# A transformer block on one core: dummy matmuls on ones at the start, tokens split straight from PSUM, and norms spread by a matrix of ones

## The chip, the cores and the metric

The kernel runs on one core of one Trainium2 chip, in one launch. The metric is device time in microseconds, the median of several executions. A profile is one further execution, recorded by the hardware profiler; its span is a little shorter than the device time of the same execution. The engines are called PE (TensorE matmul), PEld (its weight load), DVE (VectorE), ACT (ScalarE), POOL (GpSimd) and SP (SyncE, which starts DMAs).

## The reference

One transformer block over 528 tokens (16 learned meta tokens ahead of 512 real ones) of width 1024, all in float32:

```python
h = concat([meta, x])                                   # 528 x 1024
h = h + 0.5 * swiglu(rmsnorm(h, ffn1_norm), w_gate, w_up, w_down)   # d_ff = 2816
h = h + hybrid_mixer(rmsnorm(h, mix_norm))
h = h + 0.5 * swiglu(rmsnorm(h, ffn2_norm), w_gate2, w_up2, w_down2)
return rmsnorm(h, final_norm)[16:]

rmsnorm(x, g) = x * rsqrt(mean(x*x, -1) + 1e-6) * g
swiglu(u, ...) = (silu(u @ w_gate) * (u @ w_up)) @ w_down
```

The mixer projects the normed tokens with one wide matrix, runs a retention of 4 heads (keys of 256, values of 512, each head's output normed by its own root mean square, then gated) and an attention of 8 heads over 16 meta tokens and 128 keys chosen by an index score, gates and adds both, and projects them back.

## The kernel before

**Layout.** Activations lie with the features on the partitions and the tokens along the free dimension, so 1024 features are 8 tiles `hT[k]` of 128 x 528. Every matmul is made of three: each float32 operand is split into a `hi` part rounded to the PE's float32r form and a `lo` part with the rest, and `mm3` issues hi x hi, hi x lo and lo x hi for each of the 8 slices. ACT makes the `hi` part and another engine (DVE, if nothing else is said) the `lo` part, once for each weight (`split_w`, 1024 columns per partition) and once for each activation tile (`split`, or `split_gain`, which multiplies by the norm's gain on the way). A product over 528 tokens is issued in two parts (`halves`), each in a bank of its own of a two-bank PSUM tile. There are four such tiles in the first feed-forward stage.

**Norms.** The gain is folded into the activations as they are split; the factor per token is applied behind the product, when a PSUM tile is read: `R` is a 128 x 528 tile with the token's factor on every partition. `rstd_steps` makes it. It is a generator, so that its caller can put other matmuls between its steps: (1) PE sums `ssum` (the squares, already added over the 8 tiles by DVE or POOL) over the partitions by matmuls against a column of ones, which gives one column per 128 tokens; DVE scales it and POOL raises it to the power -0.5, which gives `rcol`; (2) PE transposes `rcol` and DVE copies the rows out, which gives `rrow`; (3) PE multiplies, for each 128 tokens, a column of the identity, broadcast, by these rows, which puts a row's factors on all partitions; ACT copies the result out of PSUM. The function is called seven times: for the first norm (`psr`), for the mixer's (`psn`, R2), for the output of each of the four retention heads (`rn`), and for the norm of the second feed-forward stage (R3).

**The start.** SP loads the tokens in five pieces by rows of tokens (`xt0` to `xt4`; sides[0] is the first 256 tokens, sides[1] the other 272) and, between them, the first two gate weights of 128 columns each. `token_half(h, k0)` transposes two feature slices of one side into a PSUM tile, copies both to `hT` (ACT or DVE in turn), and splits them from there. The first side's four pairs come first; then PE goes through the first gate tile's eight slices for the first 256 tokens, and after every second slice it transposes a pair of the second side. The two weights' `lo` parts are made by POOL here. Then the squares of all `hT` are added up, the second gate tile is run for the first 256 tokens, both tiles for the other 272, and the first up tile begins (`psu`), with the three steps of the norm between its parts. From there the two feed-forward halves (12 and 10 tiles of 128 hidden features) run gate, up and down.

**Order.** PE's instructions go in the order of the program text. The instructions of the other engines are ordered by a scheduler when the program is built, from its own estimate of when each is ready, and are then issued in that fixed order. Each engine waits on semaphores where it needs another's result. Tiles of one `tag` share a number of buffers (`bufs`), and a new tile waits until the oldest user of its buffer is done. `tmp()` is such a shared scratch tile of 128 x 528; the norm's callers in the mixer already use it.

Of the kernel before, what the change touches and what calls it, by code (L numbers as in the profile page):

```python
# [18 lines left out]
P = 128  # L19
D = 1024  # L20
KD = D // P
S = 512
# [59 lines left out]
def kernel(ctx: ExitStack, tc: tile.TileContext, x, meta, g1, wg1, wu1, wd1, gm,  # L82
# [11 lines left out]
    def pool(name, bufs=1, space=None, side=None):  # L94
        kw = {} if space is None else {"space": space}
        if side is not None:
            kw["side"] = side
        return tc.tile_pool(name=name, bufs=bufs, reuse_waits="tile", **kw)
# [7 lines left out]
    make_identity(nc, ident)  # L106
    ones = cpool.tile([P, 1], F32, name="ones")
    nc.gpsimd.memset(ones, 1.0)
    mhalf = cpool.tile([P, 5], F32, name="mhalf")
    nc.gpsimd.memset(mhalf, -0.5)  # L110
    gains = cpool.tile([P, 3, KD], F32, name="gains")
# [68 lines left out]
    def xs(k):  # L180
        return xs_now[k]
# [3 lines left out]
    def halves(t, cut=TH):  # L185

        a, b = t[:, 512 - cut : 512], t[:, 512 : 512 + T - cut]
        return [(a, slice(0, cut)), (b, slice(cut, T))], t[:, 512 - cut : 512 - cut + T]

    def rstd_steps(ssum, n, dim, dst, sp, psum):  # L190

        ends = [min(b * P, n - P) for b in range(-(-n // P))]
        nb = len(ends)
        col = psum()
        for b, t0 in enumerate(ends):
            nc.tensor.matmul(col[:, b : b + 1], ssum[:, t0 : t0 + P], ones, start=True, stop=True)
        ms = sp.tile([P, 5], F32, tag="ms", name="ms", bufs=2)
        nc.vector.tensor_scalar(ms[:, :nb], col[:, :nb], 1.0 / dim, EPS, ALU.mult, ALU.add)
        r = sp.tile([P, 5], F32, tag="rcol", name="rcol", bufs=2)
        nc.gpsimd.tensor_tensor(r[:, :nb], ms[:, :nb], mhalf[:, :nb], ALU.pow)  # L200
        yield True
        rows = psum()
        nc.tensor.transpose(rows[:nb, 0:P], r[:, :nb], ident)
        rs = sp.tile([5, P], F32, tag="rrow", name="rrow")
        nc.vector.tensor_copy(rs[:nb, :], rows[:nb, 0:P])
        yield True
        ps = psum()
        for b, t0 in enumerate(ends):
            t1 = min(b * P + P, n)
            nc.tensor.matmul(ps[:, b * P : t1], ident[:nb, b : b + 1].to_broadcast([nb, P]), rs[:nb, b * P - t0 : t1 - t0],  # L210
                             start=True, stop=True)
        nc.scalar.activation(dst, ps[:, :n], AF.Copy)  # L212
        yield False

# [24 lines left out]
    with pool("f1") as fp, pool("f1ps", 4, PSUM) as mmp:  # L239
        def mm_tile(name):  # L240
            return mmp.tile([P, 1024], F32, tag="mm", name=name)
# [8 lines left out]
            nc.tensor.transpose(pg[:, : n * KD], grow[n - 1], ident[: n * KD, : n * KD])  # L250
            nc.vector.tensor_copy(gains[:, i : i + n, :].rearrange("p a k -> p (a k)"), pg[:, : n * KD])

        hT2 = [fp.tile([P, 2, T], F32, tag=f"hT{k}", name=f"hT{k}") for k in range(KD // 2)]
        hT = [hT2[k // 2][:, k % 2, :] for k in range(KD)]
        sides = [[(0, P), (P, P)], [(2 * P, P), (3 * P, P), (4 * P, NM)]]
        bounds = [b for side in sides for b in side]
        sts = ExitStack()
        st_pool = sts.enter_context(pool("st"))
        xt, first_raw = [], []
        for b, (t0, n) in enumerate(bounds):  # L260
            t = st_pool.tile([n, D], F32, tag=f"xt{b}", name=f"xt{b}")
# [9 lines left out]

        CUT0 = 2 * P

        def token_half(h, k0):
            hs = (slice(0, CUT0), slice(CUT0, T))[h]
            w = hs.stop - hs.start
            ps = mm_tile("pst").rearrange("p (a b) -> p a b", a=2)
            for k in (k0, k0 + 1):
                for b, (t0, n) in enumerate(sides[h]):
                    nc.tensor.transpose(ps[:, k % 2, b * P : b * P + n], xt[2 * h + b][:, k * P : (k + 1) * P],  # L280
                                        ident[:n, :n])
            pair = hT2[k0 // 2][:, :, hs]
            if k0 % 4:
                nc.scalar.activation(pair, ps[:, :, :w], AF.Copy)
            else:
                nc.vector.tensor_copy(pair, ps[:, :, :w])
            for k in (k0, k0 + 1):
                xh, xl = xs(k)
                split_gain(hT[k][:, hs], gains[:, 0, k : k + 1], xh[:, hs], xl[:, hs])

        for k in range(KD):
            new_x(k)
        gains_in(0, 1)
        for k in range(0, KD, 2):
            if k == 0:
                first_w = split_w(first_raw[0], nc.gpsimd)
            token_half(0, k)
        pss = [mm_tile("psg") for _ in range(1)]
        for k in range(KD):
            mm3(halves(pss[0], CUT0)[0][:1], [w[:, k : k + 1, :] for w in first_w], lambda _: xs(k), 1, k == 0, k == KD - 1)  # L300
            if k % 2:
                token_half(1, k - 1)
            if k == 1:
                next_w = split_w(first_raw[1], nc.gpsimd)
        sts.close()
        hidp = sts.enter_context(pool("hid"))
        ssum = fp.tile([P, T], F32, tag="ssum", name="ssum")
        for k in range(KD):
            add_square(hT[k], ssum, k == 0, fp, bufs=4, eng=nc.vector)

        for f0, nf in ((0, 12), (12, 10)):
            hid = []
            for f in range(f0, f0 + nf, 2):
                cg = slice(f * P, (f + 2) * P)
                if f:
                    raw = load_w(wg1[:, cg], KD, 2 * P)
                    pss = []
                    for i in range(2):
                        w = split_w(raw[:, :, i * P : (i + 1) * P])
                        ps = mm_tile("psg")  # L320
                        mm3(halves(ps)[0], w, xs, KD)
                        pss.append(ps)
                else:
                    pss.append(mm_tile("psg"))
                    mm3(halves(pss[1], CUT0)[0][:1], next_w, xs, KD)
                    for p_, w in zip(pss, (first_w, next_w)):
                        mm3(halves(p_, CUT0)[0][1:], w, xs, KD)
                    psr = mm_tile("psr")
                    norm = rstd_steps(ssum, T, D, R, fp, lambda: psr)
                    raw = load_w(wu1[:, cg], KD, 2 * P)  # L330
                    w0 = split_w(raw[:, :, :P])
                    ps0 = mm_tile("psu")
                    part = halves(ps0)[0]
                    mm3(part[:1], [w[:, :4, :] for w in w0], xs, 4, True, False)
                    next(norm)
                    mm3(part[:1], [w[:, 4:, :] for w in w0], lambda k: xs(k + 4), 4, False, True)
                    mm3(part[1:], [w[:, :4, :] for w in w0], xs, 4, True, False)
                    next(norm)
                    mm3(part[1:], [w[:, 4:, :] for w in w0], lambda k: xs(k + 4), 4, False, True)
                    next(norm)  # L340
                st = []
                for i in range(2):
                    t = fp.tile([P, T], F32, tag="t", name="t", bufs=3)
                    nc.vector.tensor_tensor(t, halves(pss[i], TH if f else CUT0)[1], R, ALU.mult)
                    nc.scalar.activation(t, t, AF.Silu)  # L345
                    nc.gpsimd.tensor_tensor(t, t, R, ALU.mult)  # L346
                    st.append(t)
                if f:
                    raw = load_w(wu1[:, cg], KD, 2 * P)
                for i in range(2):  # L350
                    if f + i == 0:
                        ps = ps0
                    else:
                        w = split_w(raw[:, :, i * P : (i + 1) * P])
                        ps = mm_tile("psu")
                        mm3(halves(ps)[0], w, xs, KD)
                    if f + i == 1:
                        gains_in(1, 2)
                    pr = fp.tile([P, T], F32, tag="pr", name="pr", bufs=2)
                    nc.vector.tensor_tensor(pr, halves(ps)[1], st[i], ALU.mult)  # L360
                    hh = hidp.tile([P, TX], F32R, tag=f"hh{f - f0 + i}", name="hh")[:, :T]
                    hl = hidp.tile([P, TX], F32R, tag=f"hl{f - f0 + i}", name="hl")[:, :T]
                    split(pr, hh, hl)
                    hid.append((hh, hl))
# [38 lines left out]

    def mm_tile(name):
        return mmp.tile([P, 1024], F32, tag="mm", name=name)

    tp = {}

    def tmp():
        return tp["pool"].tile([P, T], F32, tag="tmp", name="tmp", bufs=tp["bufs"])  # L410

    def rope_swap(ps, cos, sin, half, n):

# [479 lines left out]
    ssum3 = hpool.tile([P, S], F32, tag="ssum3", name="ssum3")  # L893
    R3 = hpool.tile([P, S], F32, tag="R3", name="R3")
    with pool("om") as ou:
        def to_tokens(c, hc):
            ps = sm_tile("psht")
            for b in range(4):
                nc.tensor.transpose(ps[:, b * P : (b + 1) * P], hc[:, b * P : (b + 1) * P], ident)
            for b in range(4):  # L900
                nc.scalar.activation(hTok[b][:, c * P : (c + 1) * P], ps[:, b * P : (b + 1) * P], AF.Copy)
# [150 lines left out]
```

## Time and profile before

| | |
|---|---|
| median of 3 runs | 1612.23 us (1612.2 to 1612.44) |
| profiled execution | 1612.07 us, span 1610.2 us |
| mean granted PE clock | 0.994 |
| PE | 1590.3 us busy (99%), 9772 matmuls |
| DVE, ACT, POOL | 816.0, 564.7 and 238.9 us busy (51%, 35%, 15%) |
| DMA | 148.66 MB, mean 92 GB/s |
| instructions | 23061 |

How the views are read. The page's strip shows the span in 40 slices, one digit each; the clock digit is the share of full TensorE speed that was granted. A table of windows gives, for each stretch of time, each engine's busy time and instruction count, the granted clock and the DMA. The chain is the work that ended last, followed back from the end: each piece was released by the one before it. A group line gives line, engine, operation, output and inputs, shapes and count, then busy time and the mean duration of one in ns, then the idle time before it and who ended it. The duration of a pipelined matmul is longer than its distance to the next, so paces are taken from a piece of the chain divided by its count. In names, `whi` and `wlo` are a weight's two parts, `xh` and `xl` an activation tile's, `pst` a PSUM tile of transposed tokens, and `psg`, `psu`, `psd` products of gate, up and down.

### The profile page before, as it was taken

The numbers are of one execution on the slowest core, as the hardware profiler recorded it, in microseconds if no ns is written. First come the engines' busy times: TensorE is split into PE (matmuls) and PEld (weight loads), VectorE is DVE, ScalarE is ACT, GpSimd is POOL, SyncE is SP. The second block draws the span as 40 slices with busy tenths as digits, with TensorE's granted clock in tenths as the row PEclk, the third lists the DMA queues.
The fourth block names the chain that finished last, engine by engine and source line by source line (L and its number), as shares of the span: only waits on it lengthen the run. The fifth ranks groups of instructions, "written<-read, shape, count | busy, mean of one in ns | idle before, by whom it ended". The sixth has DMA issues, their size and how long they took to land.

```text
span 1610.2 us, 23061 instructions
## 1 busy us (share of the span) xinstructions
PE 1590.3 (99%) x9772; PEld 1429.6 (89%) x9772; DVE 816.0 (51%) x1256; ACT 564.7 (35%) x897; POOL 238.9 (15%) x186
## 2 busy tenths in 40 slices
PE   7999999999999999999999999999999999999998
PEld 6999999999888889889888999988888888888886
DVE  4333333334485686776844667653454343333434
ACT  4322222224543323233233555553234332212323
POOL 2111001101320200301303300111002211001100
PEclk7999999999999999999999999999999999999999
DMA  5232233224342032231312422222343323233222
GB/s 165 80 101 70 90 108 98 87 66 149 100 136 69 27 128 66 80 101 53 119 52 66 119 66 66 83 76 82 102 137 99 110 87 105 79 106 104 92 84 86
DMA packets 148262, 148.66 MB, mean 92 GB/s; under 512 B 3224, under 2 KB 137392, under 8 KB 148160
## 3 DMA queue, kind: packets, MB, share of 16 engines
q1 hardware_dynamic: 143632, 138.23, 26.8%
q10 hardware_dynamic: 4464, 8.96, 1.6%
q8 instruction: 76, 1.25, 0.3%
q14 instruction: 26, 0.21, 0.0%
q0 software_dynamic: 64, 0.01, 0.0%
HBM read 143.00 MB, written 4.19 MB: 91 GB/s over the span
## 4 chain that ended last, share of the span: by engine, by line
PE 95%; DVE 2%; DMA 1%; ACT 1%; POOL 1%; issue 1%; SPq 0%; ACTq 0%; POOLq 0%; DVEq 0%
PE psg L150 16%; PE psu L150 15%; PE psd L150 8%; PE psd L1013 7%; PE psrv L150 6%; PE psrg L150 5%; PE psro L150 4%; PE psrk L150 3%; PE psrq L150 3%; PE psgate L150 3%; PE psmo L150 3%; PE psat L150 3%; PE psga L150 3%; PE psak L150 3%; PE psav L150 3%; PE psaq L150 2%
## 5 line engine op out<-in xcount | busy, mean ns | idle before, releaser
L115 ACT ACTIVATE whi<-raw 128x1024 fp32r<-128x1024 f32 (+3 forms) x283 | 277.7, 982 | 875.3 <-PE psu L150 171.7
L116 DVE TENSOR_TENSOR wlo<-raw,whi 128x1024 fp32r<-128x1024 f32 (+3 forms) x281 | 336.0, 1196 | 176.5 <-ACT whi L115 172.9
L150 PE MATMUL psg<-xl,whi 128*128 128x264 f32 (+3 forms) x528 | 144.1, 323 | 1.9 <-DVE xl L120 1.9
L150 PE MATMUL psg<-xh,whi 128*128 128x264 f32 (+3 forms) x528 | 145.5, 325 | 0.4 <-ACT xh L119 0.4
L150 PE MATMUL psg<-xh,wlo 128*128 128x264 f32 (+3 forms) x528 | 143.9, 322 | 0.0
L150 PE MATMUL psu<-xh,whi 128*128 128x264 f32 (+1 forms) x528 | 141.4, 319 | 0.7 <-ACT R L212 0.7
L150 PE MATMUL psu<-xl,whi 128*128 128x264 f32 (+1 forms) x528 | 140.6, 318 | 0.0
L150 PE MATMUL psu<-xh,wlo 128*128 128x264 f32 (+1 forms) x528 | 140.4, 318 | 0.0
L150 PEld LDWEIGHTS psg<-xl,whi 128*128 128x128 f32 x528 | 90.9, 192 | 8.9 <-DVE xl L120 2.1
L150 PEld LDWEIGHTS psg<-xh,whi 128*128 128x128 f32 x528 | 90.1, 192 | 7.6 <-ACT xh L119 0.6
L150 PEld LDWEIGHTS psg<-xh,wlo 128*128 128x128 f32 x528 | 90.5, 192 | 6.9
L150 PEld LDWEIGHTS psu<-xh,whi 128*128 128x128 f32 x528 | 87.5, 188 | 7.8 <-ACT R L212 0.8
L150 PEld LDWEIGHTS psu<-xl,whi 128*128 128x128 f32 x528 | 88.1, 188 | 6.8
L150 PEld LDWEIGHTS psu<-xh,wlo 128*128 128x128 f32 x528 | 87.8, 188 | 6.9
L346 POOL TENSOR_TENSOR t<-t,R 128x528 f32<-128x528 f32 x22 | 37.5, 1708 | 263.8 <-ACT t L345 263.8
L988 POOL TENSOR_TENSOR t<-t,R 128x512 f32<-128x512 f32 x22 | 38.1, 1735 | 253.4 <-ACT t L987 253.4
L150 PE MATMUL psd<-hh,whi 128*128 128x264 f32 x352 | 71.3, 284 | 0.0
L150 PE MATMUL psd<-hl,whi 128*128 128x264 f32 x352 | 70.8, 283 | 0.0
L150 PE MATMUL psd<-hh,wlo 128*128 128x264 f32 x352 | 70.6, 282 | 0.0
L1013 PE MATMUL psd<-whi,hh 128*128 128x512 f32 x176 | 68.5, 389 | 0.0
L1013 PE MATMUL psd<-wlo,hh 128*128 128x512 f32 x176 | 68.5, 389 | 0.0
L1013 PE MATMUL psd<-whi,hl 128*128 128x512 f32 x176 | 68.5, 389 | 0.0
(304 smaller groups left out, 3512.5 us busy)
## 6 DMA issues: line engine op xcount, KB each, us to landing
raw<-in_w_in_dram SPq DMA_DIRECT2D x34, 1024.0 KB, 4.9
raw<-in_ffn_w_up_dram SPq DMA_DIRECT2D x22, 1024.0 KB, 5.0
raw<-in_ffn_w_gate_dram SPq DMA_DIRECT2D x21, 1024.0 KB, 5.0
raw<-in_w_in_dram SPq DMA_DIRECT2D x25, 512.0 KB, 3.4
raw<-in_ffn_w_down_dram SPq DMA_DIRECT2D x10, 1024.0 KB, 4.8
raw<-in_w_ret_out_dram SPq DMA_DIRECT2D x16, 512.0 KB, 3.3
raw<-in_ffn_w_down_dram SPq DMA_DIRECT2D x8, 768.0 KB, 4.3
raw<-in_ffn_w_down_dram SPq DMA_DIRECT2D x8, 640.0 KB, 3.9
```

What stands on the lines that cost most here:

```text
L115: nc.scalar.activation(hi, src, AF.Copy)
L116: eng.tensor_tensor(lo, src, hi.bitcast(F32), ALU.subtract)
L150: nc.tensor.matmul(o, a[:, k, :], b[:, sl], start=first and k == 0 and i == 0, stop=last and k == nk - 1 and i == 2)
L346: nc.gpsimd.tensor_tensor(t, t, R, ALU.mult)
L988: nc.gpsimd.tensor_tensor(t, t, R, ALU.mult)
L1013: nc.tensor.matmul(pss[b], a[:, bs], m[:, k % 2, :], start=k0 + k == 0 and i == 0, stop=k0 + k == nf - 1 and i == 2)
```

## The change

- A tile `idle` of ones (128 x 512) is filled by DVE at the start, and `keep_busy(n)` issues n matmuls of 512 columns on it into a PSUM tile that nobody reads: ten before the gains and the tokens, two between the first side's two groups of transposes, and one each before the slices 0, 1 and 2 of the first gate tile.
- `token_parts(h, k0, n)` replaces `token_half`: it transposes n slices (four at a time for the first side, two for the second), splits `xh` and `xl` straight from PSUM, and copies the tokens to `hT` afterwards, in one instruction for the n slices.
- The two first weights' `lo` parts are made by DVE in place of POOL.
- The second side's first two pairs are transposed behind slices 3 and 5 of the first gate tile, the other two behind slices 1 and 3 of the second gate tile, whose first part now runs slice by slice too.
- `rstd_steps`: step 2 is empty. In step 3, DVE multiplies the identity by `rcol` into a row of diagonal blocks (128 x 528 or 128 x 512), ACT and DVE split it, and PE multiplies a 128 x 128 matrix of ones by both parts, 512 columns at a time. Three `tmp` tiles are used for this, in every stage that runs a norm.
- `gap` tiles and a shared `tmp` in the first stage shift where tiles lie in memory; `rrow` goes.

```diff
+    ones_r = cpool.tile([P, P], F32R, name="ones_r")
+    nc.gpsimd.memset(ones_r.bitcast(F32), 1.0)
...
     def rstd_steps(ssum, n, dim, dst, sp, psum):
...
         nc.gpsimd.tensor_tensor(r[:, :nb], ms[:, :nb], mhalf[:, :nb], ALU.pow)
         yield True
-        rows = psum()
-        nc.tensor.transpose(rows[:nb, 0:P], r[:, :nb], ident)
-        rs = sp.tile([5, P], F32, tag="rrow", name="rrow")
-        nc.vector.tensor_copy(rs[:nb, :], rows[:nb, 0:P])
         yield True
+        diag, hi, lo = (tmp() for _ in range(3))
+        hi, lo = hi.bitcast(F32R), lo.bitcast(F32R)
+        nc.vector.tensor_tensor(diag[:, :S].rearrange("p (b c) -> p b c", b=4),
+                                ident.unsqueeze(1).to_broadcast([P, 4, P]),
+                                r[:, :4].unsqueeze(2).to_broadcast([P, 4, P]), ALU.mult)
+        if n > S:
+            nc.vector.tensor_scalar(diag[:, S:n], ident[:, P - (n - S) :], r[:, 4:5], None, ALU.mult)
+        split(diag[:, :n], hi[:, :n], lo[:, :n])
         ps = psum()
-        for b, t0 in enumerate(ends):
-            t1 = min(b * P + P, n)
-            nc.tensor.matmul(ps[:, b * P : t1], ident[:nb, b : b + 1].to_broadcast([nb, P]), rs[:nb, b * P - t0 : t1 - t0],
-                             start=True, stop=True)
+        for c0 in range(0, n, S):
+            cs = slice(c0, min(c0 + S, n))
+            for i, part in enumerate((hi, lo)):
+                nc.tensor.matmul(ps[:, cs], ones_r, part[:, cs], start=i == 0, stop=i == 1)
         nc.scalar.activation(dst, ps[:, :n], AF.Copy)
...
+        idle = st_pool.tile([P, 512], F32R, tag="idle", name="idle")
+        nc.vector.memset(idle.bitcast(F32), 1.0)
...
+        def keep_busy(n):
+            for _ in range(n):
+                nc.tensor.matmul(spare[:, :512], idle[:, :P], idle, start=True, stop=True)
+
+        def token_parts(h, k0, n):
             hs = (slice(0, CUT0), slice(CUT0, T))[h]
             w = hs.stop - hs.start
+            ps = mm_tile("pst").rearrange("p (a b) -> p a b", a=n)
+            for k in range(n):
+                for b, (t0, rows) in enumerate(sides[h]):
+                    nc.tensor.transpose(ps[:, k, b * P : b * P + rows], xt[2 * h + b][:, (k0 + k) * P : (k0 + k + 1) * P],
+                                        ident[:rows, :rows])
+            for k in range(n):
+                xh, xl = xs(k0 + k)
+                split_gain(ps[:, k, :w], gains[:, 0, k0 + k : k0 + k + 1], xh[:, hs], xl[:, hs])
+            kept = hT4[k0 // 4][:, k0 % 4 : k0 % 4 + n, hs]
+            if k0 % (2 * n):
+                nc.scalar.activation(kept, ps[:, :, :w], AF.Copy)
             else:
+                nc.vector.tensor_copy(kept, ps[:, :, :w])
+
+        spare = mm_tile("idle")
+        keep_busy(10)
         for k in range(KD):
             new_x(k)
         gains_in(0, 1)
-        for k in range(0, KD, 2):
-            if k == 0:
-                first_w = split_w(first_raw[0], nc.gpsimd)
-            token_half(0, k)
-        pss = [mm_tile("psg") for _ in range(1)]
+        token_parts(0, 0, 4)
+        first_w = split_w(first_raw[0])
+        keep_busy(2)
+        token_parts(0, 4, 4)
+        pss = [mm_tile("psg")]
+
+        def first_half(i, w, k):
+            mm3(halves(pss[i], CUT0)[0][:1], [p[:, k : k + 1, :] for p in w], lambda _: xs(k), 1, k == 0, k == KD - 1)
+
         for k in range(KD):
-            mm3(halves(pss[0], CUT0)[0][:1], [w[:, k : k + 1, :] for w in first_w], lambda _: xs(k), 1, k == 0, k == KD - 1)
-            if k % 2:
-                token_half(1, k - 1)
-            if k == 1:
-                next_w = split_w(first_raw[1], nc.gpsimd)
+            if k < 3:
+                keep_busy(1)
+            first_half(0, first_w, k)
+            if k in (3, 5):
+                token_parts(1, k - 3, 2)
+            if k == 3:
+                next_w = split_w(first_raw[1])
+        pss.append(mm_tile("psg"))
+        for k in range(KD):
+            first_half(1, next_w, k)
+            if k in (1, 3):
+                token_parts(1, k + 3, 2)
         sts.close()
         hidp = sts.enter_context(pool("hid"))
+        tp.update(pool=fp, bufs=3)
+        gap(fp, 16)
...
-                    pss.append(mm_tile("psg"))
-                    mm3(halves(pss[1], CUT0)[0][:1], next_w, xs, KD)
```

More of the change, by code (lines that the diff above doesn't have):

```diff
@@ L188, in halves, with tmp @@
         return [(a, slice(0, cut)), (b, slice(cut, T))], t[:, 512 - cut : 512 - cut + T]
+    tp = {}
+    def tmp():
+        return tp["pool"].tile([P, T], F32, tag="tmp", name="tmp", bufs=tp["bufs"])
     def rstd_steps(ssum, n, dim, dst, sp, psum):
@@ L251, in gains_in @@
             nc.vector.tensor_copy(gains[:, i : i + n, :].rearrange("p a k -> p (a k)"), pg[:, : n * KD])
-        hT2 = [fp.tile([P, 2, T], F32, tag=f"hT{k}", name=f"hT{k}") for k in range(KD // 2)]
-        hT = [hT2[k // 2][:, k % 2, :] for k in range(KD)]
+        hT4 = [fp.tile([P, 4, T], F32, tag=f"hT{k}", name=f"hT{k}") for k in range(KD // 4)]
+        hT = [hT4[k // 4][:, k % 4, :] for k in range(KD)]
         sides = [[(0, P), (P, P)], [(2 * P, P), (3 * P, P), (4 * P, NM)]]
@@ L272 @@
         CUT0 = 2 * P
-        def token_half(h, k0):
+        def keep_busy(n):
+            for _ in range(n):
+                nc.tensor.matmul(spare[:, :512], idle[:, :P], idle, start=True, stop=True)
+        def token_parts(h, k0, n):
             hs = (slice(0, CUT0), slice(CUT0, T))[h]
             w = hs.stop - hs.start
[L277 to L284, printed above, removed]
-            else:
[L286 to L289, printed above, removed]
+            ps = mm_tile("pst").rearrange("p (a b) -> p a b", a=n)
[9 more added lines that the diff above has]
+                nc.scalar.activation(kept, ps[:, :, :w], AF.Copy)
+            else:
+                nc.vector.tensor_copy(kept, ps[:, :, :w])
+        spare = mm_tile("idle")
+        keep_busy(10)
         for k in range(KD):
@@ L405, in mm_tile @@
         return mmp.tile([P, 1024], F32, tag="mm", name=name)
-    tp = {}
-    def tmp():
-        return tp["pool"].tile([P, T], F32, tag="tmp", name="tmp", bufs=tp["bufs"])
     def rope_swap(ps, cos, sin, half, n):
@@ L895 @@
     with pool("om") as ou:
+        tp.update(pool=ou, bufs=3)
         def to_tokens(c, hc):
```

## The prediction

> **What bounds the kernel now.** I read the page first, then the clock by stage, then the chain of waits of the first 45 us, then the chain around each norm.
>
> ```profile
> PE 1590.3 (99%) x9772; PEld 1429.6 (89%) x9772; DVE 816.0 (51%) x1256; ACT 564.7 (35%) x897; POOL 238.9 (15%) x186
> PEclk7999999999999999999999999999999999999999
> PE 95%; DVE 2%; DMA 1%; ACT 1%; POOL 1%; issue 1%; SPq 0%; ACTq 0%; POOLq 0%; DVEq 0%
> ```
>
> TensorE carries 95% of the chain that ended last, so an instruction taken from PE's stream is taken from the time, and one put on DVE or ACT costs nothing unless PE comes to wait for it. Only the first of 40 slices has a lower clock. By stage (us, then busy time and instructions of PE, PEld, DVE, ACT, POOL, then the granted clock and the DMA):
>
> ```profile
> 2.60:6.00 3.40, 0.39 (x2) 0.32 (x2) 0.17 (x1) 0.00 (x0) 0.69 (x6) 1.00 0.94 286
> ...
> 9.50:12.90 3.40, 1.08 (x6) 0.65 (x6) 3.25 (x3) 3.40 (x9) 2.36 (x1) 1.00 0.85 250
> 12.90:30.00 17.10, 17.10 (x72) 14.15 (x72) 9.93 (x21) 10.90 (x22) 2.59 (x2) 0.50 0.41 139
> 30.00:36.00 6.00, 6.00 (x50) 6.00 (x49) 4.73 (x6) 2.37 (x3) 0.00 (x0) 1.00 0.00 0
> ```
>
> PE is idle for two thirds of 9.5 to 12.9; at 12.9 the clock falls to 0.50 and stays there for 17.1 us in which PE never rests. Those 17.1 us are what the start can win from. The chain shows what they hold (start, length, what):
>
> ```profile
> 8.85 1.06 ACT whi L115
> ...
> 10.34 2.30 DVE xl L120
> ...
> 12.68 1.29 PE psg L150 x5
> 13.97 1.47 PE pst L280 x6
> ...
> 24.60 11.46 PE psg L150 x72
> 36.06 1.44 PE psu L150 x12
> ...
> 43.06 1.23 PE psr L210 x10
> ...
> 44.31 0.62 ACT R L212
> ...
> 44.97 1.12 PE psu L150 x7
> ```
>
> The first gate weight is split from 8.85, the first lo part of a token tile (xl) takes 2.30 us, and only at 12.68 does PE get its second matmul. From there it alternates six matmuls with six transposes until the last 72 matmuls end at 36.06, where the up projection begins. I call that point S: the start's gain is how much earlier S comes.
>
> **The start.** First, the durations of its pieces (line, engine, shape, count, busy us, mean ns, idle before):
>
> ```profile
> L116 POOL TENSOR_TENSOR wlo<-raw,whi 128x1024 fp32r<-128x1024 f32 x2 | 4.7, 2360 | 12.6 <-ACT whi L115 12.6
> L116 DVE TENSOR_TENSOR wlo<-raw,whi 128x1024 fp32r<-128x1024 f32 x2 | 2.4, 1222 | 0.4 <-ACT whi L115 0.4
> L119 ACT ACTIVATE xh<-hT,gains 128x256 fp32r<-128x256 f32 x8 | 3.5, 498 | 0.0
> L120 DVE SCALAR_TENSOR_TENSOR xl<-hT,gains,xh 128x272 fp32r<-128x272 f32 x8 | 3.6, 497 | 2.2 <-ACT xh L119 2.2
> L286 DVE COPY hT<-pst 128x512 f32<-128x512 f32 x2 | 1.4, 692 | 5.8 <-PE pst L280 5.8
> ```
>
> What starts when, from the timeline, and PE's wait from the table of waits:
>
> ```profile
> 0.74 0.20 POOL masks.py:197 MEMSET ident<- 128x128 f32 x1 [0.29 <-POOLq L1038]
> 6.89 3.10 PE L280 MATMUL pst<-ident,xt 128*128 128x128 f32 x15 [0.57 <-DMA xt<-in_x_dram]
> PE psg L150 <- DVE xl L120: 1.9, 1, 1.9
> ```
>
> And rows for PE's pace at full clock, in their order of time:
>
> ```profile
> 166.58 69.12 PE psd L150 x576
> ...
> 593.67 0.51 PE psvt L659 x4
> ...
> 1070.54 16.62 PE psgate L150 x72
> ...
> 1150.65 43.52 PE psat L150 x192
> ```
>
> So at full clock a 264-column matmul takes 69.12/576 = 0.120 us, a 512-column one 43.52/192 = 0.227, a transpose 0.51/4 = 0.13.
>
> *Ones.* Ten 512-column matmuls at half clock are about 10 x 0.45 = 4.5 us, from some 1.3 (engines start at 0.74, and DVE fills the tile first) to 5.8. PE is otherwise idle there (0.39 us in the row 2.60:6.00), and the tokens' transposes stay where the DMA puts them (all but the first from 6.89), so they cost nothing on the path. The two between the transposes and the one before k=0 also fall into PE's wait for the weight. The `spare` tile they write takes one of four PSUM tiles until k=2; the three left hold the gains, the two early token tiles and, once the gains are out, the first gate tile, so none waits. POOL's fill of ones_r (0.20, as ident's) is needed only after S. The two before k=1 and k=2 stand between real matmuls: 0.45 us if the data are there.
>
> *Tokens from PSUM, weights on DVE.* The copy to SBUF no longer stands ahead of xh. Both first weights' lo parts go from POOL (2.36 us) to DVE (1.22 us); that takes away the overlap in which the first xl took 2.30 us beside 0.50 elsewhere, as POOL ran its split in the same stretch. New is that DVE has it all: 16 xl at about 0.45, the two weights 2.4, the hT copies it keeps (one of 1024 columns, about 1.2 at 692 ns for 512, and two of 0.7), 12 us in all; started at about 8.5 they end by 21, if nothing waits. The seven additions for the norm come behind, before S + 1.4. When is k=0 complete? The weight still lands at 8.85; ACT 1.06, DVE 1.22, one xl 0.50 and hand-overs: between 11.7 and, with the 1.2 us copy put ahead, 12.9. I take 12.0, because ACT began with the weight in the chain above too. That is hardly before 12.68: the gain is not here.
>
> *PE's work from 12.0 to S at full clock:* two tiles' first parts, 48 matmuls of 256 columns at 0.120 = 5.8; four pairs of transposes, each 4 x 0.13 + two short ones, so about 1.0 where half clock took 1.47, = 4.0; ones 0.45; second parts, 48 matmuls of 272 columns at 0.125 (the row 30.00:36.00 fits 48 of them) = 6.0. Sum 16.3, S = 28.3.
>
> *The clock.* Full clock all through is not what I expect. Between the last early transposes (6.89 + 15 x 0.13 + two ones 0.45 = 9.3) and 12.0 PE has one ones matmul and two real ones, about 0.5 us of 3.4; the same stretch before held 1.08 us and was followed by half clock. So I expect it again at about 12.9. What differs is what follows: PE then has k=1, 2, 3 and two ones matmuls at half clock in a row, some 3 us without a transpose, where before transposes with gaps came after 1.29 us. The clock returned at 30.0 after such an unbroken stretch (24.60 on). I take 3.4 us, the length of the stretch from 9.5 to 12.9, as the length of one spell: half clock from 12.9 to 16.3, which costs 1.7. S = 30.0, a gain of 6.1.
>
> Here a rule bears on it. The Trainium skill, "TensorE: Matmul & The Clock Gate", in Part 1 and in its closing table, says the gate watches free-running windows of about 3.4 us and falls back to half after a window of idleness, with the advice to leave no idle gap over about 3 us. By that rule the ones matmuls keep every gap under 3 us and the clock never falls: rival A below, 1598.8. The trace disagrees in part: PE's longest wait in that stretch was 1.9 us, and the clock fell.
>
> **The norms.** `rstd_steps` runs seven times. Its PE part, before:
>
> ```profile
> 420.59 0.11 PE psn L203
> 426.15 1.21 PE psn L210 x10
> ...
> 548.11 0.11 PE psn L203
> 554.73 1.08 PE psn L210 x8
> ...
> 873.43 1.08 PE psn L210 x8
> ...
> 1253.39 0.12 PE psn L203
> ...
> 1253.96 1.12 PE psn L210 x8
> 1255.09 7.03 PE psu L150 x30
> ```
>
> And when the powers come (timeline, POOL):
>
> ```profile
> 1248.10 1.94 POOL L200 TENSOR_TENSOR rcol<-ms,mhalf 128x4 f32<-128x4 f32 x1 [3.35 <-DVE ms L198]
> 38.87 2.06 POOL L200 TENSOR_TENSOR rcol<-ms,mhalf 128x5 f32<-128x5 f32 x1 [18.07 <-DVE ms L198]
> ```
>
> The transpose and 8 or 10 small matmuls go; two 512-column matmuls by ones come, 2 x 0.227 = 0.45 (0.51 with the two 16-column ones). On DVE and ACT come a diagonal (0.69, as the copy of 512 columns), its hi part (0.62, as R's copy) and its lo part (0.69): 2.0 us, ready that long after `rcol`. PE's first matmul by ones is the instruction that would wait for it, with the next weight's matmuls behind it in PE's queue.
> - Mixing norm: 0.11 + 1.21 - 0.51 = 0.8 saved. between its two rows lies a projection of 5.5 us, and another lies ahead of the first.
> - Four heads: 0.11 + 1.08 - 0.45 = 0.74 each, 3.0. Between sums and spreading lie two key projections, or two of the last head's output tiles, 5.5 us by 24 matmuls at 0.23; power and spreading take at most 2.1 + 2.0.
> - Last norm: PE went from 1253.39 to 1255.09, 1.70, with a wait for `rrow`. `rcol` was there at 1250.04, the split diagonal would be by 1252.2, before PE comes: 0.45 instead, 1.25 saved.
> - First norm: `rcol` at 40.93, plus 2.2 is 43.1, when PE comes there: about no wait, 0.51 instead of 1.23, so R and the matmul behind it 0.5 earlier. With a weight's 1.22 ahead on DVE it is 0.7 later.
> Sum 5.5. The end below: if DVE is late each time and PE waits as long as it saved, 0; below that I see no reason, as DVE has idle time near every one. The end above 6. I take 5.5.
>
> **Sum.** The profiled execution took 1612.07 (span 1610.2, 1.87 around it), 0.16 under the median. 1612.07 - 6.1 - 5.5 = 1600.5.
>
> **The rivals.**
> - A, the clock never falls back: S 28.3, a gain of 7.8 + 5.5, 1598.8. For it: the ones matmuls. Against: the stretch before 12.0 is as empty as the one that lost the clock. The skill's rule would give this.
> - B, the clock falls and stays down until the second parts, as before: a 256-column matmul at half clock is (11.46 - 48 x 0.125)/24 = 0.23 by the chain's last 72, so PE needs 48 x 0.23 + 4 x 1.47 + 0.9 = 17.8, to 29.8, then 48 x 0.125: S 35.8, 1606.3. For it: 17.1 us of busy PE did not bring the clock back.
> - C, the norms give nothing since PE waits for the diagonals: 1606.0.
> - D, slower: the new tiles (ones_r, idle, three tmp) move other tiles to other addresses, and matmuls go at the pace of `psgate` (16.62/72 = 0.231) instead of `psat` (0.227), 1.8%. On all of PE's 1590.3 us that is 28.6: 1629. It decides from 11.6/1590 = 0.7% on. For it: the trace has both paces for the same shape. Against: most tiles already keep within 0.3%, and the slower ones lie beside busy DVE.
>
> **How the numbers follow.** Forecast 0.40, A 0.25, B 0.13, C 0.10, D 0.12, of which 0.04 near no change and 0.08 slower. A measurement here tells 0.2% (3.2 us) from nothing. Range: below A by 1 us for norms at their upper end, up to B and C: 1597.5 to 1606.5, leaving out D and the tail of the others. Faster 0.88, same 0.04, slower 0.08.
>
> **What would show it.** Right: ones matmuls from about 1.3 us; the psu chain beginning near 30 with a half-clock spell of about 3.4 us; no L203 or L205, and two ones_r matmuls of 0.45 us per norm without a wait; psu of the last stage some 1.2 us sooner after the sums. Wrong: half clock beyond 17 us, PE waiting on `lo` of a diagonal, or a mean above 0.120 and 0.227 us for the long chains.

## The result and the profile after

The changed kernel takes 1600.2 us (median of 4 executions, 1600.08 to 1601.56) against 1612.22 us for the kernel before beside it (4 executions, 1611.35 to 1612.44): ratio 0.9928, 95% interval 0.9911 to 0.9946. The forecast was 1600.5. Two more measurements of the same kernel gave 1600.37 and 1600.22. The profiled execution took 1601.56 us, the longest of the four, with a span of 1599.7 (before 1610.2).

The page of the kernel after: busy time by engine, the clock in 40 slices, and the engines of the chain that ended last.

```profile
PE 1584.3 (99%) x9738; PEld 1423.4 (89%) x9738; DVE 826.7 (52%) x1267; ACT 568.7 (36%) x903; POOL 232.3 (15%) x186
PEclk9999999999999999999999999999999999999999
PE 92%; DVE 3%; ACT 2%; issue 1%; POOL 1%; DMA 1%; SPq 0%; ACTq 0%; POOLq 0%; DVEq 0%
```

PE has only 6.0 us less busy time, while 10.5 us are gone. The first slice has its clock back: 9 in place of 7. The chain through ACT and DVE has not become shorter but a little longer (DVE 3%, ACT 2%; 2% and 1% before). The start of the kernel after, by stretches of 3.41 us (busy time and instructions of PE, PEld, DVE, ACT, POOL, then the granted clock, the DMA share and GB/s):

```profile
5.25:8.66 3.41, 2.76 (x19) 2.06 (x19) 0.47 (x2) 1.76 (x2) 0.00 (x0) 1.00 1.01 352
8.66:12.08 3.42, 1.47 (x10) 0.95 (x9) 1.71 (x3) 1.78 (x3) 0.00 (x0) 1.00 1.02 333
12.08:15.49 3.41, 3.41 (x15) 2.88 (x14) 3.11 (x7) 2.71 (x5) 0.00 (x0) 0.50 0.77 247
15.49:18.90 3.41, 3.25 (x22) 2.44 (x21) 2.28 (x4) 1.70 (x5) 1.00 (x1) 1.00 0.42 153
18.90:22.32 3.42, 2.53 (x16) 1.96 (x17) 3.17 (x5) 3.42 (x7) 0.00 (x0) 1.00 0.80 254
```

The clock falls once, at 12.08, for one stretch of 3.41 us, where it was down for 17.1 before. From 18.90 on it is ACT that has no pause (3.42 of 3.42), and PE has one. The chain of the kernel after shows the same (start, length, what):

```profile
9.46 1.06 ACT whi L117
...
10.55 1.24 DVE wlo L118
...
13.72 1.35 PE psg L152 x6
...
18.06 0.86 ACT xh L121 x2
18.92 0.95 ACT whi L117
19.87 0.91 ACT hT L307
...
23.20 1.13 PE pst L300 x6
24.33 7.69 PE psg L152 x60
32.02 1.44 PE psu L152 x12
```

From 18 to 23 the path runs through ACT. S, the start of the up projection, is 32.02 (before 36.06): 4.04 gained, not 6.1. The norms' pieces of the chain, then DVE's timeline ahead of the last one:

```profile
549.92 0.48 PE psn L223 x2
...
1244.36 0.46 PE psn L223 x2
1244.82 10.89 PE psu L152 x48
```

```profile
1241.02 0.69 DVE L213 TENSOR_TENSOR tmp<-ident,rcol 128x512 f32<-128x512 f32 x1 [0.92 <-POOL rcol L208]
1242.42 0.69 DVE L118 TENSOR_TENSOR tmp<-tmp 128x512 fp32r<-128x512 f32 x1 [0.70 <-ACT tmp L117]
```

Two matmuls by ones take 0.46 and begin as the last projection ends, 1.3 us after the split diagonal is ready. So the 10.5 us between the two profiles are: 4.04 at the start; 6.23 between S and the last stage's `psu` (1255.09 - 36.06 = 1219.03 before, 1244.82 - 32.02 = 1212.80 after); 0.2 behind it. Of the 6.23, two rows of the tables of waits explain 1.3 net that is not a norm's own work (waited for: us in total, times, longest). Before:

```profile
PE psst L622 <- DVE tmp L626: 2.6, 2, 1.5
...
PE psrg L150 <- DVE wlo L116: 0.2, 1, 0.2
```

After:

```profile
PE psrg L152 <- DVE wlo L118: 0.9, 2, 0.6
...
PE psst L650 <- DVE tmp L654: 0.6, 1, 0.6
```

`psst`, the scores of the retention, waited 2.0 us less; `psrg`, a gate projection, 0.7 more. The norms' own work is about 4.9 of the 6.23.

### The profile page after: what moved, and what is told of

Same layout as the page of the kernel before. It is cut to its first block, busy times and chain, and to the rows that moved or that the text cites. A ratio compares the mean times of both kernels' runs of the same rounds, so it can differ in the third digit from the quotient of the medians.

```text
span 1599.7 us, 23001 instructions
## 1 busy us (share of the span) xinstructions
PE 1584.3 (99%) x9738; PEld 1423.4 (89%) x9738; DVE 826.7 (52%) x1267; ACT 568.7 (36%) x903; POOL 232.3 (15%) x186
## 4 chain that ended last, share of the span: by engine, by line
PE 92%; DVE 3%; ACT 2%; issue 1%; POOL 1%; DMA 1%; SPq 0%; ACTq 0%; POOLq 0%; DVEq 0%
PE psu L152 15%; PE psg L152 15%; PE psd L152 8%; PE psd L1042 7%; PE psrv L152 6%; PE psrg L152 5%; PE psrk L152 3%; PE psak L152 3%; PE psav L152 3%; PE psgate L152 3%; PE psro L152 3%; PE psmo L152 3%; PE psaq L152 3%; PE psat L152 3%; PE psga L152 3%; PE psrq L152 2%
```

## The experiments

The theory was the prediction's: the ones buy the start's gain through the clock, the norms give what PE no longer issues. The rivals: the token order gives the start's gain and the ones nothing; or the norms' gain is something else. A further question followed from the trace of after: why S was 2 us late. All runs in one table. "Down" is the half-clock time inside the start, after the clock had first been full ("until" is when it first became full, given where that came after 11 us); `psu` 2 is the start of the last stage; the waits are those of `psst`.

| run | S | down | psu 2 | psst | median us | ratio to before, 95% |
|---|---|---|---|---|---|---|
| before | 36.06 | 12.88 to 29.95 | 1255.09 | 2.6 | 1612.2 | |
| after | 32.02 | 12.08 to 15.49 | 1244.82 | 0.6 | 1600.20 | 0.9911 to 0.9946 |
| after_again | 30.45 | none | 1243.18 | 0.7 | 1600.37 | 0.9919 to 0.9947 |
| after_third | 30.43 | none | 1243.19 | 0.8 | 1600.22 | 0.9919 to 0.9943 |
| e1 no ones | 33.45 | until 21.88 | 1247.57 | 1.2 | 1604.80 | 0.9938 to 0.9966 |
| e2 old norms | 31.34 | until 11.08 | 1250.31 | 1.4 | 1607.73 | 0.9957 to 0.9980 |
| e3 new norms only | 34.65 | 13.29 to 26.95 | 1248.75 | 1.2 | 1605.66 | 0.9933 to 0.9965 |
| e4 more ones | 30.55 | none | 1247.48 | 3.7 | 1604.21 | 0.9929 to 0.9959 |
| e4b, the same | 35.02 | 19.31 to 29.56 | 1250.20 | 2.1 | 1604.09 | 0.9942 to 0.9972 |
| e5 before + ones | 28.66 | none | 1246.09 | 0.5 | 1603.27 | 0.9949 to 0.9981 |
| e6 lo parts on POOL | 30.64 | none | 1243.40 | 0.7 | 1601.99 | 0.9934 to 0.9970 |
| e7 e5 + new norms | 34.47 | 14.21 to 27.86 | 1247.25 | 0.7 | 1603.94 | 0.9930 to 0.9958 |
| e8 e7 + PSUM source | 33.99 | 10.39 to 13.80, 24.04 to 27.46 | 1250.32 | 2.3 | 1604.92 | 0.9949 to 0.9973 |
| e9 e4 + SBUF source | 27.87 | none | 1243.51 | 2.0 | 1598.38 | 0.9906 to 0.9931 |

S, the clock and the waits are those of the one profiled execution of each, the medians those of 4 to 11 executions, and whether the clock fell differs among these (below). e1 to e4 shared one chip, after_again and e4b to e6 another, after_third and e7 to e9 a third; ratios go by the runs of before on the same chip (medians 1612.99, 1611.76, 1611.49).

**e1, the change without its ones.**

```diff
-        spare = mm_tile("idle")
-        keep_busy(10)
...
-        keep_busy(2)
...
-            if k < 3:
-                keep_busy(1)
```

> The changed kernel (1600.2 us) without any of the 15 matmuls on ones; all else as changed. Clock theory: without them PE starts at half clock, may get one spell of full clock from the tokens' transposes and then loses it while it waits for the first weight, and stays at half clock well past 15.5 us, since transposes come between; the up projection begins about 3 us later than the changed kernel's 32.0: 1603 to 1605. Rival, that the shorter path (split from PSUM, weights on DVE, two tiles) earns the start's gain and the ones nothing: 1600 within 0.5. Third, that the ones only delay: faster than 1600.

The chain of e1:

```profile
16.25 1.58 PE psg L152 x6
...
33.45 1.44 PE psu L152 x12
```

The clock first became full at 21.88. The views count the clock only from there on (the mean of e1 is 0.999), so the half clock ahead of it is read from the pace: six gate matmuls take 1.58 us, as in the half-clock stretch of before (15.44 on), and 0.91 in after_third. S was 33.45: 3.0 us later than in the two runs of the change in which the clock never fell (30.43 and 30.45), and the median is 4.4 to 4.6 us above theirs, on another chip. So the ones carry about half of the start's 5.6 us in this order. The other 2.6 came without them: the clock was full from 21.88 and not from 29.95.

**e2, the change with the old norms; e3, the old start with the new norms.** e2 puts the old body of `rstd_steps` back into the kernel after; e3 puts the old start (`token_half`, POOL's lo parts, no ones) into it.

> The changed kernel with rstd_steps as it was before (transpose, row copy, small matmuls), the start as changed. If the norms give what PE's chain shows (0.5 first, 0.8 mixing, 0.74 per head, 1.25 last, and a lost wait for a PSUM tile), 5.5 to 6.5 us slower than the changed kernel: about 1606. If the norms give nothing and the start all 12 us: 1600.

> The kernel before with only the new rstd_steps (and its three scratch tiles), the start as before. Norms theory: 1612.2 less 5.5 to 6.5, about 1606, so that both halves add up to the whole. Rival, that the norms pay only behind the new start: about 1612.

Both halves give time by themselves: 5.3 us and 7.3 us less than before by the medians of the same chip. (e2 is 1.7 us above its forecast: its S is 0.9 later than in after_again, and its `psst` waits 0.7 longer.) The norms are read best from S to `psu` 2, less the `psst` waits, since the start is then out of it. With the old norms that is 1216.4 (before), 1217.6 (e2) and 1216.9 (e5). With the new ones it is 1212.0 to 1213.2 in nine runs (1212.2 in the kernel after), and 1213.6 and 1214.0 in e9 and e8, where the clock was down for another 3.41 us in between (from 693.22 and from 805.70). Without these two the differences reach from 3.2 to 5.6; the pair that differs in the norms alone, e2 and after, gives 5.4. The wait on `psrg`, 0.2 in before, e2 and e5, is 0.8 or 0.9 in all eleven runs with the new norms, whatever their start: it came with them. In the early window of e3, another thing shows: its start is the old one but its clock returned one stretch of 3.41 us sooner (26.95 against 29.95, having fallen at 13.29 against 12.88). S 34.65 in place of 36.06 need not be an effect of the norms, whose first step comes behind S.

**e4, seven ones ahead of k=0, none ahead of k=1 and 2; e4b, the same kernel measured again; after_again.**

```diff
-            if k < 3:
-                keep_busy(1)
+            if k == 0:
+                keep_busy(7)
```

> The changed kernel with seven ones matmuls before slice 0 of the first gate tile and none before slices 1 and 2 (1, 1 and 1 as changed): they fill PE's wait from 8.9 to 10.5 us. Theory that too little PE work in that stretch makes the clock fall at 12.1: no half-clock spell from 12 to 15.5, PE's alternation 1 to 1.7 us earlier, 1598.5 to 1599.5. Rival, that ACT and DVE set the pace from 18 to 23 us anyway, so that the spell costs nothing: the spell goes and the time stays at 1600.2. Second rival, that the fall doesn't depend on the amount of work: the spell stays.

> The kernel with seven ones matmuls before slice 0 again, beside the changed one. In its first profile the half-clock spell was gone and the up projection began at 30.4, 1.6 us sooner, but 3.1 us more were lost at the retention scores, behind a weight that landed late. If that landing is chance, the median is 1 to 1.6 us below the changed kernel's here; if the earlier start always meets that wait, the medians are equal or this one's is higher.

> The changed kernel once more, so that the others of this batch stand beside it on the same chip, and to see how far its start and its later waits vary from one profiled execution to another: the up projection to begin between 30.5 and 32, the wait at the retention scores (0.6 us in the first profile) between 0.6 and 3.7, the ratio to the kernel before again 0.992 to 0.994.

In e4 the clock was full from 7.66 on, and yet S was 30.55, not 28.3: a full clock was not what S lacked. `psst` then waited 3.7 us, 3.0 more than in after_again, and the median of 1604.21 missed the forecast of 1598.5 to 1599.5. e4b repeats it: 1604.09, 3.7 us above after_again on the same chip. In its profile the clock fell at 19.31 for 10.24 us (window of e4b, columns as above, and its chain):

```profile
15.90:19.31 3.41, 2.40 (x15) 1.60 (x14) 3.25 (x6) 2.45 (x5) 0.50 (x1) 1.00 0.35 96
```

```profile
35.02 1.44 PE psu L152 x12
```

PE was busy for 2.40 of the 3.41 us before the fall, though its matmuls cover less (below). after_again had no fall at all, S 30.45. So the spell of 3.41 us in the profile of after is one execution's, not the kernel's.

**e5, the kernel before with ones: 10 first and 8 ahead of the first gate tile; e6, the change with the first weights' lo parts on POOL.**

```diff
+        spare = mm_tile("idle")
+        keep_busy(10)
         for k in range(KD):
             new_x(k)
...
+        keep_busy(8)
         pss = [mm_tile("psg") for _ in range(1)]
```

> The kernel before with ones matmuls alone: ten at the start, eight between the first side's transposes and the first gate tile; tokens, weights, order and norms as before. Clock theory: no half-clock spell or a short one, and the 17 us of PE work at half clock shrink; the up projection starts near 31 to 32 instead of 36.1, time 1607.5 to 1609. Rival, that the order and the splits from PSUM carry the start's gain: 1612.

> The changed kernel with the two first weights' lo parts made by POOL, as before. If POOL's 2.36 us for 1.22 and its clash with DVE cost what the chain before showed (first xl 2.3 us for 0.5): k=0 complete 1.1 to 1.8 us later, 1 to 2 us slower than the changed kernel. If ACT paces the start and DVE gains 2.4 us of free time: the same or up to 1 us faster.

e5 was the surprise: the old token order with ones came to the up projection at 28.66, earlier than the change in any of its runs. Its chain:

```profile
12.35 0.91 PE psg L150 x5
...
19.61 9.05 PE psg L150 x72
28.66 1.45 PE psu L150 x12
```

From 12.35 on PE never waits: 16.3 us, close to the sum that the prediction had made for PE at full clock. The ones alone were worth 7.4 us in this execution, and S is 1.8 later with the change's token order. e6 shows that it isn't the lo parts' engine: there k=0 was complete at 12.69, 2.0 us later than in after_third, and S came only 0.2 later (30.64). So something behind k=0 sets S in the change. e6's median is 1.6 us above after_again's; three of its eight executions took 1605.92 to 1608.01 us at a mean granted clock of 0.993 to 0.994.

**e7, e8, e9 and after_third: which part of the token order costs.** e7 is e5 with the new norms. e8 is e7 with the split from PSUM and the copy behind it; e9 is e4 with the copy put back first and the split from `hT`:

```diff
             for k in range(n):
                 xh, xl = xs(k0 + k)
-                split_gain(ps[:, k, :w], gains[:, 0, k0 + k : k0 + k + 1], xh[:, hs], xl[:, hs])
...
+            for k in range(n):
+                xh, xl = xs(k0 + k)
+                split_gain(hT[k0 + k][:, hs], gains[:, 0, k0 + k : k0 + k + 1], xh[:, hs], xl[:, hs])
```

> The order of before at the start (tokens copied to SBUF and split from there, the first weights' lo parts on POOL), with 10 ones matmuls first and 8 more ahead of the first gate tile, and the new norms. If the ones carry the whole gain of the start and the split from PSUM takes part of it back: up projection from about 28.5 us as in the other run with before's order and ones (28.7 by its chain), the norms' 5 to 6 us behind it, some 13 us less span than before, a time of 1598 to 1599, at or below the changed kernel. If the change's token order is worth something of its own: up projection not before 30, and a time above the changed kernel's by 1 us or more.

> As the run with before's order, ones and the new norms, but xh and xl read the transposes' PSUM tile, and the copy for the norm comes behind them. If it is the PSUM source that costs (ScalarE and VectorE taking turns on one tile): up projection about 1.5 to 2 us later than in that run, at 30 to 30.5, and the time 1.5 to 2 us above it. If it is the change's spread of the late transposes over two gate tiles and its four-at-once tiles: no later than 28.7, and the same time.

> The changed kernel with 7 ones ahead of the first gate matmul (none between the next two) and the copy to SBUF put back ahead of xh and xl. If the PSUM source costs: up projection at 28.5 to 29.2, against 30.4 in the run with the PSUM source and full clock. If the spread over two gate tiles costs: 30.4 or later, since the 1024-column copy now stands ahead of the first split.

> The changed kernel unchanged, on the chip of the other three. 1600.2 within 1 us if the two earlier medians (1600.2 and 1600.4) are its time; up projection at 30.3 without a half-clock spell, near 32 with one of 3.4 us.

e9 against e4 is the clean pair (both at full clock all through the start, one edit apart): S 27.87 against 30.55. The split from PSUM, with the copy behind it, costs 2.7 us. S of e4 in its chain:

```profile
30.55 1.44 PE psu L152 x12
```

The chain of after_third (the change, full clock), and ACT's timeline there:

```profile
11.14 0.48 ACT xh L121
...
11.65 0.49 DVE xl L122
...
12.17 0.48 ACT xh L121
...
16.48 0.87 ACT xh L121 x2
17.35 0.95 ACT whi L117
18.30 0.92 ACT hT L307
...
22.74 7.69 PE psg L152 x60
30.43 1.44 PE psu L152 x12
```

```profile
9.36 0.82 ACT L121 ACTIVATE xh<-pst,gains 128x256 fp32r<-128x256 f32 x2
11.14 0.87 ACT L121 ACTIVATE xh<-pst,gains 128x256 fp32r<-128x256 f32 x2 [0.96 <-DVE xl L122]
```

and the same of e9, the chain and then ACT:

```profile
11.37 1.69 PE psg L152 x11
...
20.18 7.69 PE psg L152 x60
27.87 1.44 PE psu L152 x12
```

```profile
9.57 1.69 ACT L121 ACTIVATE xh<-hT,gains 128x256 fp32r<-128x256 f32 x4
```

With the PSUM source ACT stops for 0.96 us between two `xh` of one tile until DVE has read it for `xl`, and the path alternates ACT, DVE, ACT, DVE. With the SBUF source ACT makes four `xh` in a row, PE's one wait for the splits (0.43 us) ends at 11.37, and from there on the chain is PE's alone. The Trainium skill, "PSUM — Partial Sum Buffer", section "PSUM bank collisions raise a hardware error", says that two engines must not touch one bank at once, reads among them. The turns in the trace are wider than that: the `xh` at 11.14 is slice 2's, in the tile's second bank (a slice has 256 columns, a bank 512), and waits for the `xl` of slice 1, in the first. Whether tiles of one bank each would do without this wait was not run.

The turns are only a part of the 2.7 us. Two rows of after_third's table of waits show another, which e9 doesn't have:

```profile
PE psg L152 <- DVE hT L309: 0.9, 1, 0.9
...
PE pst L300 <- ACT hT L307: 0.2, 1, 0.2
```

A gate matmul reads nothing of `hT`; what it waits for is a PSUM tile. The copy to `hT` now stands behind the splits, so a tile of transposes is held until it is done, and the second gate tile and the last transposes wait for one. Laid side by side, PE's timelines of e4 and e9 differ by 1.2 us in slices 1 to 3, by 1.5 in the 12 matmuls up to the second gate tile's slice 1 (0.9 of it this wait), and by 0.3 at the last transposes, while e9 had begun slice 1 0.45 later. No run parts the source from the place of the copy.

e8 and e7 can't be compared by S as expected, since the clock fell in both, differently. e8 does show the waits that e7 hasn't: one of its transposes waited 2.6 us for DVE's copy, and the gate matmuls 1.5 us for ACT's, and its two falls in the start come at these waits. e7 missed its forecast of 1598 to 1599 in the median, and its median is 3.7 us above the change's on the same chip. In its profile the clock fell, and stayed down until the stretch in which only matmuls run (window and chain of e7):

```profile
10.79:14.21 3.42, 2.02 (x14) 1.44 (x12) 3.12 (x5) 2.57 (x6) 1.25 (x1) 1.00 0.65 164
```

```profile
23.32 11.16 PE psg L152 x72
34.47 1.44 PE psu L152 x12
```

The mean granted clock of its six executions splits their times: 0.999 in two of 1598.31 and 1598.69 us, 0.994 to 0.995 in four of 1603.8 to 1604.82. e5 does the same: 0.999 with 1601.42 to 1603.04 us in five, 0.993 to 0.994 with 1609.36 to 1611.52 in four, and two between. The change had 0.998 once and 0.999 to 1.000 in its other 13 executions. So the old order with ones and the new norms (e7) is faster than the change only where the clock holds, and it often doesn't. The mean says this only of kernels whose clock is full early: before has 0.993 to 0.999 on the chip of e7, with 1610.01 to 1613.15 us and no such split.

e9 has the lowest median, 1598.38 us (1597.89 to 1600.26) where the change took 1600.22 (1599.86 to 1600.93) on the same chip. That is 1.8 us, 0.11%, under the 0.2% taken as the bound, and the two ranges overlap, so it isn't shown to be faster. Its start is 2.6 us better in the profiles, but its profiled execution, the slowest of its five, lost this again: `psst` waited 1.2 us longer, and a half-clock spell came behind it. In the profile of e9 (window, then DVE):

```profile
689.80:693.22 3.42, 1.37 (x17) 1.15 (x16) 3.25 (x7) 1.00 (x3) 0.00 (x0) 1.00 0.02 7
```

```profile
689.97 1.23 DVE L118 TENSOR_TENSOR wlo<-raw,whi 128x1024 fp32r<-128x1024 f32 x1 [2.28 <-ACT whi L117]
691.11 0.08 DVE L533 MATCH_VALUE_LOAD score<-top,score 128x8 f32 x1
691.18 0.54 DVE L533 MATCH_REPLACE8 score<-top,score 128x384 f32<-128x384 f32 x1
691.64 1.51 DVE L654 TENSOR_TENSOR tmp<-psst,u 128x512 f32<-128x512 f32 x3
```

DVE's queue holds a weight's lo part ahead of the `tmp` that frees a `psst` tile, and waits 2.28 us for ACT to make the hi part; PE waits 2.0 us behind it, and the clock then goes down from 693.22 to 696.64. The waits of `psst` vary among runs from 0.5 to 3.7 us, longer where DVE waits longer for the weight's hi part (0.69 us in e5, 2.41 in e4). What sets the time of that weight wasn't settled. It is where an earlier start can be lost again: e4 and after_again had nearly the same S and are 4.3 us apart at `psu` 2, 3.0 of it at `psst`.

## Why the prediction was right, point by point

- **Ones: right.** They began at 1.46, and the two runs at full clock (before's order, 36.06 to 28.66; the change's order, 33.45 to 30.43) show what they bring. The early ones cost nothing on the path: in e5 PE still waits 1.5 us for `xl` behind them. The two between k=0, 1 and 2 stood on it with 0.43 each in the profile of after, 0.86 in all at half clock, where the forecast had 0.45 for both at full clock.
- **k=0 complete at 12.0: right by luck** in the profile (the weight's lo part at 11.79). The weight landed at 9.44, 0.6 later than forecast, and the path behind it was 2.35 us, not 3.15, as `xl` was done before the weight came. In after_third, where ACT had the weight at 8.44, it was 10.72.
- **PE's work of 16.3 us from there: the sum is nearly right and the premise failed.** PE alone needs 16.3 (e5) or 16.5 us (e9, 11.37 to 27.87). That has no ones in it, and the forecast's sum without its two is 15.8; six transposes and the six matmuls behind them took 1.82 us in both, 0.1 more than forecast, four times. In the change it took 19.7 (after_third, 10.72 to 30.43), since PE waits for ACT and DVE. The step that failed is "12 us in all; started at about 8.5 they end by 21, if nothing waits": it added DVE's pieces, and left out that ACT and DVE take turns on a PSUM tile and that the copy behind the splits holds that tile. DVE's last `xl` ends at 25.25 in after_third, PE's last wait for ACT at 21.6, and the price is the 2.7 us between e4 and e9. The copy to SBUF that no longer stands ahead of `xh` was thought to save something; ahead, it is cheaper.
- **The clock: the mechanism right, its certainty wrong.** One spell, 3.41 us long, at 12.08 (forecast 3.4 from 12.9) came in the profiled execution. It did not come in after_again and after_third. The forecast S of 30.0 thus met the usual 30.4 by two errors that cancel: 1.7 too much for a spell that is rare, 2.1 too little for PE's waits. In the profiled execution, which had both, S was 32.02. That the time came out at 1600.2 for 1600.5 is luck of the same kind: the forecast is 6.1 for the start and 5.5 behind it, after_again has 5.6 and 6.3, of which 2 or so are shorter waits at `psst`.
- **Norms: right mechanism, a little too much.** Forecast 5.5; after against e2 5.4, after against before 4.2 (6.23 less the 2.0 of `psst`). The forecast saw DVE's work only in the norms' own waits, which did not come. It did not see the 0.7 at `psrg`, where a weight's lo part now comes late on DVE. The 2.0 us less wait at `psst` was in no term.
- **A**, the clock never falls, is what the clock did in two of the change's three profiles, and its 1598.8 did not come, because S was then not 28.3. It came near with e9, where the PSUM source is gone. **B**, the clock stays down until the second parts, did not happen in the change, but it did in e7 and e4b (S 34.47 and 35.02 against B's 35.8): one fall among the transposes is enough for it. **C** is false, by e2 and e3. **D** is false: the down projection of the first half runs at the pace of before.

```profile
162.06 69.12 PE psd L152 x576
```

## What to carry to other kernels

Where the clock is lost at a start, put dummy matmuls on the engine first and look at it before reordering anything: ones alone, in the old order, brought S to 28.66 where the clock held, and the new order on top of them cost 1.8 us there. Measure it more than once: by the granted clock it was down for long in four of 11 executions of e5 and in four of six of e7, and for short in one of 14 of the change as it stands. A copy that two engines then read side by side from SBUF can be cheaper than two engines that take turns on PSUM, and it frees the PSUM tile sooner. Sum each engine's pieces, and then also ask which of them may run at the same time.

## What the runs showed of the hardware that was not expected

The half-clock spells are whole multiples of 3.413 us: 17.07 in before (5), 3.41 in after (1), 13.65 in e3 and e7 (4), 10.24 in e4b (3). They lie on a grid whose offset differs among executions of one kernel (the clock became full at 5.25, 6.05 and 5.94 in three of the change). The Trainium skill, "TensorE: Matmul & The Clock Gate", Part 1, calls the windows free-running; the traces agree. By its closing table a window of idleness is what throttles. There the traces say more: PE was never idle for a whole window. Its longest single waits ahead of the falls in the start were 1.9 us (before), 1.2 (after), 1.4 (e7), 0.9 (e4b) and 2.6 (e8).

What separates the windows that lost the clock is how much of them the matmuls' streams fill. I counted each matmul as its columns at the full-clock pace (0.227 us for 512, twice that at half clock), and a transpose as two passes. Over the 14 traces, from 2 us to 1585 us, with the grid of each, the nine windows that were followed by a fall were filled to less than 0.4, and the more than 6400 that were not, to 0.41 or more. The count and the bound are fitted to these traces, and a kernel made to sit at the bound was not run. For the return no bound is shown. The windows that brought the clock back were filled to about 0.8 or more and most of the others to less, but with each stream laid from the start of its record, or from the end of the one before, one that brought it back has 0.76 (before, 6.06 to 9.47) and one that didn't 0.81 (e1, from 8.23). A fill that is too low would explain two riddles of the prediction. PE was busy without a pause from 12.88 in before, and the clock stayed down, in stretches with six transposes to six matmuls, which fill to 0.77 to 0.79. And the 3.41 us before it came back, 26.54 to 29.95, were matmuls alone.
